# A hybrid DeltaNet, spatial-gating and Fourier step on one core: operations queued in written order, and the output's loads and end reordered

## The chip, the cores and the metric

The kernel runs on one core of one Trainium2 chip. The metric is the device time of one execution in microseconds (us). Its engines are TensorE (PE, its weight loads PEld), VectorE (DVE), ScalarE (ACT), GpSimd (POOL) and SyncE (SP), which only issues DMAs. Each engine works through a queue of its own in a fixed order, and waits on semaphores for the others.

## The reference

One layer of a backbone with three token mixers. It is run for 128 context tokens (the prompt) and 2048 latent tokens (the sample); `D_MODEL` is 1024, the branches are 512 wide, everything is float32.

```python
def mixer(xn, w_in, conv_w, ...):
    proj = jnp.einsum('btd,de->bte', xn, w_in)
    qkv, beta, dec, z_a, u_b, v_b, z_b, x_c, z_c, gates = jnp.split(proj, points, axis=-1)
    ...  # short conv and silu on qkv, l2norm of q and k, beta and decay
    o, s_f, s_b = delta_bidir(q, k, v, g, beta, s0_f, s0_b)   # chunks of 64, both directions
    o = rmsnorm(o, o_norm_g) * jax.nn.silu(z_a)
    o_b = chunk_sgu(u_b, v_b, sgu_norm_g, w_spatial, b_spatial) * jax.nn.silu(z_b)
    o_c = fourier_mix(x_c, grid) * jax.nn.silu(z_c)
    br = jnp.stack([o_a, o_b, o_c], axis=2)
    pb = jnp.einsum('btnw,nwd->btnd', br, w_branch)
    gt = jax.nn.sigmoid(gates.reshape(B, T, N_BRANCH, D_MODEL))
    merged = jnp.einsum('btnd,btnd->btd', gt, pb)
    return jnp.einsum('btd,de->bte', merged, w_out), s_f, s_b

def reference(...):
    # for each group: adaLN, xn = rmsnorm(h) * (1 + scale) + shift
    out, s_f, s_b = mixer(xn, ...)
    h = h + gate * out
    y = rmsnorm(h, final_g)
    # outputs: y_prompt, y_sample, the final states of the prompt's two scans
```

In `delta_bidir` each chunk needs the solution with a unit lower triangular matrix; the state is carried from chunk to chunk.

## The kernel before, in words

**Numbers.** Every large matrix product is three fp16 products: each operand is split into a high and a low part (`hi`, `lo`) after scaling by a power of two. A weight block is loaded as float32 (`wst`), then `converting` makes it: a square with a running sum on ScalarE (L309, whose elementwise result in `w.lo` is thrown away), a cast of the sum on VectorE (L258), a matmul with ones that spreads it over the partitions, the power of two from its exponent (L271 to L273, VectorE), the high part on ScalarE (L321) and the low part on VectorE (L322). The generator yields between these, so that other work is written in between. L309 occurs 81 times: 52 blocks of 1024 columns per partition, 24 branch blocks of 512, 4 blocks of the spatial branch and one small one.

**Stages.** In the trace: adaLN and the normalised input, up to 145 us; the qkv product with its convolution, to 410; the spatial branch's v, to 520; its u and z units, to 745; the Fourier branch, to 1045; then merges 1, 2 and 0 (a gate product, a branch product, a sigmoid and a sum each), to 1345, 1682 and 1986; the output product, final norm and stores, to the end. Beside these run, in pieces handed out by `pace` between the pieces of the large products, first the preparation of the delta branch (its decays, the chunk matrices, and `base_inverse`, called five times for up to four tiles of 128 tokens), from about 432 to 880 us, and then the scan of 33 steps, from about 880 to 1670.

**Order.** The framework plans the queue of each engine: it takes the program as written, simulates its time, and puts an instruction wherever its simulation finds the engine free and the operands ready. So an instruction can come to stand ahead of others that were written before it. `tc.issue_after(ins)` adds an edge: what is written inside comes after `ins` in that engine's queue. It is no wait, only an order. `_InTurn` wraps VectorE, ScalarE and TensorE; while its `kept` is set (some parts of the start and the end), every instruction gets an edge to the one written before it. `behind_gate` does the same for some ScalarE instructions of the merges, against a gate's activation.

**The inverse.** `base_inverse(g)` loads two halves of a matrix set (SP, L1097: `ndD`, written to DRAM by earlier steps), yields eight times, copies the second half to the other partitions with its axes exchanged (L1100, VectorE), and makes 31 pairs of VectorE operations (L1107, L1108). Its result goes to DRAM after a split (L1115, L1116). Steps of other tiles are written in between, among them VectorE's reads of PSUM banks (L1058, L1063, L1074, L1077) that TensorE's transposes (L1010) filled, and fill again when they are free.

**The scan.** A step takes the state `S`, splits it into fp16 parts (`split`, L1224 on ScalarE and L1225 on VectorE), multiplies, and hands the output to `attend`: four scaled copies out of PSUM on ScalarE (L1234), later four multiply-adds on VectorE (L1241). When a direction passes from the prompt to the sample, its state is replaced by the given one, which is scaled in place (L1342, VectorE, twice in all).

**The output.** Sixteen tiles of 128 rows are worked in eight pairs (`two_tiles`); a pair takes seven products of a quarter of the size instead of eight, with sums of operands and of weights (`tw[0]` to `tw[3]`, loaded by `sums_of`). Loads of this stage are issued by SP in an order fixed by `in_turn`. The last pair and the prompt's right half (`prompt_right`) are in strict written order: `squared` (ScalarE), `final` (times the final weights), `summed_up` (VectorE), `root` (GpSimd), then the scaling by the norm and the store.

Of the kernel before, what the change touches and what calls it, by code (L numbers as in the profile page):

```python
# [168 lines left out]
class _InTurn:  # L169


    def __init__(self, tc, engine):
        self.tc, self.engine, self.kept, self.last = tc, engine, False, None

    def __getattr__(self, name):
        f = getattr(self.engine, name)
        if not self.kept:
            return f

        def call(*args, **kw):  # L180
            with self.tc.issue_after(self.last.ins) if self.last is not None else ExitStack():
                self.last = f(*args, **kw)
            return self.last

        return call


@with_exitstack
def hybrid_flow_kernel(ctx: ExitStack, tc: tile.TileContext, x_prompt, x_sample, state_delta, c, c_ctx, w_ada,
# [3 lines left out]
    G, SY = nc.gpsimd, nc.sync  # L193
    V, A, PE = [_InTurn(tc, e_) for e_ in (nc.vector, nc.scalar, nc.tensor)]
# [102 lines left out]
    def converting(w, st, nkt, cols=P, hi=None, lo=None, tag="w", bufs=5, nth=0):  # L297
# [10 lines left out]
        with behind_gate():  # L308
            w.squared = A.activation(w.lo, st, AF.Square, accum_out=ss)  # L309
# [776 lines left out]
    def base_inverse(g):  # L1086
# [13 lines left out]
        V.tensor_copy(b3(X[64:P, :]), tmp[64:P, :].rearrange("p (i j) -> p j i", j=32))  # L1100
# [126 lines left out]
    def attend(d, t, S, u, qk_, qT_):  # L1227
        o = sb(dq, [P, WB], "o")
        if S is not None:
            ps = bank(ps_out, [P, WB])  # L1230
            for h in range(H):
                mm3(ps[:, hs(h)], pair(qT_, h), pair(S, h))
            for h in range(H):
                A.activation(o[:, hs(h)], ps[:, hs(h)], AF.Copy, scale=eg[:, d, t, h:h + 1])  # L1234
# [15 lines left out]
    def scan():  # L1250
# [31 lines left out]
        for i_, (d, s_, t) in enumerate(order):  # L1282
# [46 lines left out]
            if not last:  # L1329
# [7 lines left out]
                else:  # L1337
# [4 lines left out]
                    V.tensor_scalar(S2, S2, us, FS, ALU.mult, ALU.mult)  # L1342
# [651 lines left out]
    def two_tiles(t, pa, xr, hh, end):  # L1994
# [70 lines left out]

    parts = [sb(op, [P, 3], f"part{j}", bufs=1) for j in range(3)]
# [30 lines left out]
    def prompt_right():  # L2097
# [7 lines left out]
        final(gp_right, gp_right, cols[0], slice(512, 896), V)  # L2105
# [12 lines left out]
    ahead_rows = two_rows(firsts[0], in_turn)  # L2118
    sums_of(2)
    sums_of(0)  # L2120
    sums_of(3)
# [3 lines left out]
    for i, t in enumerate(firsts):  # L2125
        rows_ = ahead_rows
        if i < 7:
            ahead_rows = two_rows(firsts[i + 1], SY.dma_start if i else in_turn)
# [39 lines left out]
```

## Time and profile before

| | |
|---|---|
| three runs | 2155.57, 2153.13, 2153.15 us (median 2153.15) |
| the profiled execution | 2157.86 us, its span 2156.0 us |
| granted TensorE clock, mean over the span | 0.992 |
| TensorE busy | 2082.2 us (97%) |
| weight loads busy | 1195.7 us |
| VectorE busy | 1360.5 us (63%) |
| ScalarE busy | 1060.6 us (49%) |
| GpSimd busy | 758.3 us (35%) |

In the views, a row of the timeline is: start, duration, engine, line, operation, result <- operands, shapes, count, and in brackets the idle time of the engine before it with what ended that. "issue" means that the profile shows nothing that was waited for. A row of the waits is: engine and line, what it waited for, us in total, times, longest. A row of windows is: from:to, length, then busy time and count of PE, PEld, DVE, ACT and POOL, then the granted clock of TensorE (1.00 is full), the DMA engines' busy share, and GB/s.

### The profile page before, as it was taken

What the parts mean: (1) busy time and instruction counts of PE and PEld (TensorE: products, weight loads), DVE (VectorE), ACT (ScalarE), POOL (GpSimd) and SP (SyncE); (2) the same over time, 40 slices, a digit from 0 to 9 for tenths busy, and PEclk for the clock granted to TensorE, in tenths of its full rate; (3) what the DMA queues carried; (4) which work ended last, traced back from release to release, by engine and by line L of the source; (5) the groups of instructions that cost most, each with busy time, mean ns of one, the idle gap of its engine ahead of it and who ended that gap; (6) DMA issues with size and microseconds to landing.
All of it is one profiled execution on the core that took longest, in us unless ns stands there. A gap on an engine that the chain in (4) does not pass through costs nothing.

```text
span 2156.0 us, 42627 instructions
## 1 busy us (share of the span) xinstructions
PE 2082.2 (97%) x16133; PEld 1195.7 (55%) x16133; DVE 1360.5 (63%) x3100; ACT 1060.6 (49%) x2457; POOL 758.3 (35%) x934
## 2 busy tenths in 40 slices
PE   7999999999899999999899999999999999999997
PEld 4455444455455587778556556555655444444443
DVE  6656854389778698556755556766665554666245
ACT  5554744476565654445544445756554353443112
POOL 0321332233343322442421233355443234333464
PEclk9999999999999999999999999999999999999999
DMA  9625732277776744444755555866664645456852
GB/s 350 220 77 195 260 109 94 82 227 220 241 231 216 223 149 118 123 125 127 225 170 158 174 162 183 261 215 208 213 199 134 206 169 175 167 196 238 336 219 88
DMA packets 222910, 403.25 MB, mean 187 GB/s; under 512 B 39720, under 2 KB 109632, under 8 KB 219888
## 3 DMA queue, kind: packets, MB, share of 16 engines
q1 hardware_dynamic: 167664, 290.84, 42.3%
q0 software_dynamic: 15216, 65.89, 8.1%
q10 hardware_dynamic: 39824, 43.79, 6.1%
q8 instruction: 127, 2.08, 0.4%
q14 instruction: 79, 0.65, 0.1%
HBM read 258.19 MB, written 142.24 MB: 186 GB/s over the span
## 4 chain that ended last, share of the span: by engine, by line
PE 52%; DVE 9%; DMA 5%; ACT 3%; issue 2%; POOL 1%; SPq 0%; ACTq 0%; POOLq 0%; DVEq 0%
PE b L244 51%; DMA st<-br 2%; DVE XB L1107 1%; DVE E L1108 1%; DMA ei<-XB 1%; DMA tw<-tw 1%; DMA br<-o 0%; DMA XB<-nd 0%; DVE sg L1447 0%; DVE big L1684 0%; DMA N<-n 0%; ACT big L1683 0%; DVE XB L1116 0%; DVE n L1077 0%; DMA S<-in_state_delta_dram 0%
## 5 line engine op out<-in xcount | busy, mean ns | idle before, releaser
L244 PE MATMUL b<-xh,whi 128*128 128x512 f16 (+1 forms) x1920 | 649.8, 347 | 4.6 <-DVE sg L1447 2.8
L244 PE MATMUL b<-xl,whi 128*128 128x512 f16 (+1 forms) x1920 | 650.3, 347 | 0.0
L244 PE MATMUL b<-xh,wlo 128*128 128x512 f16 (+1 forms) x1920 | 649.3, 347 | 0.0
L244 PEld LDWEIGHTS <-whi 128*128 128x128 f16 x3856 | 351.1, 98 | 324.3 <-issue 10.4
L244 PEld LDWEIGHTS <-wlo 128*128 128x128 f16 x1928 | 188.4, 98 | 175.2 <-issue 1.3
L244 PE MATMUL b<-big,bhi 128*128 128x512 f16 (+1 forms) x960 | 251.8, 347 | 2.3 <-ACT big L1683 1.9
L244 PE MATMUL b<-big,blo 128*128 128x512 f16 (+1 forms) x480 | 163.1, 347 | 0.0
L1727 POOL TENSOR_TENSOR mrow<-mrow,sg 128x512 f32<-128x512 f32 (+1 forms) x80 | 92.5, 1157 | 147.2 <-DVE sg L1726 106.0
L244 PEld LDWEIGHTS <-xh 128*128 128x128 f16 x1496 | 118.8, 99 | 31.0 <-DVE yT L1633 2.7
L947 POOL TENSOR_TENSOR cy<-cy,raw 128x545 f32<-128x545 f32 (+1 forms) x48 | 65.8, 1398 | 181.2 <-ACT raw L946 181.2
L244 PEld LDWEIGHTS <-bhi 128*128 128x128 f16 x960 | 86.8, 98 | 75.0 <-issue 1.0
L244 PEld LDWEIGHTS <-xl 128*128 128x128 f16 x1068 | 98.9, 99 | 45.1 <-DMA tw<-tw 2.1
L1717 ACT ACTIVATE sg<-b,winv 128x512 f32<-128x512 f32 (+1 forms) x120 | 73.9, 616 | 92.8 <-PE b L244 92.2
L244 PE MATMUL b<-whi,xh 128*128 128x128 f16 x544 | 95.2, 222 | 3.3 <-DVE yT L1633 2.5
L244 PE MATMUL b<-wlo,xh 128*128 128x128 f16 x544 | 95.2, 222 | 0.0
L244 PE MATMUL b<-whi,xl 128*128 128x128 f16 x544 | 95.2, 222 | 0.0
L322 DVE SCALAR_TENSOR_TENSOR wlo<-wst,wsc,whi 128x1024 f16<-128x1024 f32 x52 | 68.1, 1310 | 33.5 <-ACT whi L321 32.5
L1181 POOL COPY T<-ES 32x256 f16<-32x256 f16 x68 | 30.8, 454 | 161.6 <-DMA ES<-ei 150.7
L1288 POOL TENSOR_TENSOR skn<-skn,ed 128x512 f32<-128x512 f32 x34 | 39.1, 1149 | 127.8 <-DMA skn<-kv 123.2
L321 ACT ACTIVATE whi<-wst,wsc 128x1024 f16<-128x1024 f32 x52 | 59.4, 1144 | 49.2 <-DVE wsc L272 47.4
L309 ACT ACTIVATE wlo<-wst 128x1024 f16<-128x1024 f32 x52 | 54.9, 1056 | 52.1 <-DMA wst<-in_w_blk_dram 47.2
L1726 DVE SCALAR_TENSOR_TENSOR sg<-b,binv,sg 128x512 f32<-128x512 f32 (+1 forms) x80 | 53.3, 667 | 39.9 <-PE b L244 35.9
(532 smaller groups left out, 4304.2 us busy)
## 6 DMA issues: line engine op xcount, KB each, us to landing
wst<-in_w_blk_dram SPq DMA_DIRECT2D x58, 512.0 KB, 3.8
pa<-pa POOLq DMA_DIRECT2D x16, 896.0 KB, 4.4
qkv<-cy POOLq DMA_DIRECT2D x12, 1089.0 KB, 5.3
st<-br SPq DMA_DIRECT2D x48, 256.0 KB, 3.2
mrow<-mrg SPq DMA_DIRECT2D x16, 576.0 KB, 3.9
pa<-pa SPq DMA_DIRECT2D x5, 1792.0 KB, 11.3
dc<-dec SPq DMA_DIRECT2D x17, 512.0 KB, 4.6
kq<-qkv SPq DMA_DIRECT2D x34, 256.0 KB, 4.5
```

Source lines behind the costliest of these rows:

```text
L244: newest[0] = PE.matmul(out, l, r, start=start, stop=stop, skip_group_check=reopened)
L309: w.squared = A.activation(w.lo, st, AF.Square, accum_out=ss)
L321: w.made = A.activation(w.hi, st, AF.Copy, scale=s)
L322: w.low = V.scalar_tensor_tensor(w.lo, st, s, w.hi, ALU.mult, ALU.subtract)
L947: G.tensor_tensor(y[:, c0:c1], y[:, c0:c1], raw[:, 1 + c0:1 + c1], ALU.mult)
L1107: V.tensor_tensor(t3, X3[:, 0:k, k:k + 1].to_broadcast([P, k, n_]), E3[:, k:k + 1, k:32].to_broadcast([P, k, n_]), ALU.mult)
L1108: V.tensor_tensor(E3[:, 0:k, k:32], E3[:, 0:k, k:32], t3, ALU.subtract)
L1181: G.tensor_copy(T16[rows(a0, b), :, :, b], ES[0:32, :, 2 * a0 + b, :, wT])
L1288: G.tensor_tensor(h3(kn_), h3(kn_), bc(ed[:, d, t, :], P), ALU.mult)
L1717: gated_[0] = A.activation(sg, ps, AF.Sigmoid, scale=gw.inv)
L1726: V.scalar_tensor_tensor(sg, ps, binv[:, 1:2], sg, ALU.mult, ALU.mult)
L1727: G.tensor_tensor(mr, mr, sg, ALU.add)
```

## The change

`_InTurn` now remembers the newest instruction written on its engine, always, and GpSimd is wrapped as well (nothing there is queued). `queued()` gives an edge to that newest instruction. Four places use it: the weights' squares (L309, ScalarE), the copy in `base_inverse` (L1100, VectorE), `attend`'s four scaled copies (L1234, ScalarE), and the scaling of the given state (L1342, VectorE). What is written after these instructions gets no edge to them.

In the output, SP's order of loads was sums 1, rows of the first pair, sums 2, sums 0, sums 3; it is now sums 1, 2, 0, the rows, sums 3. At the end, the last pair scales and stores only its row tile 1; tile 0 is scaled and stored in `prompt_right`, after the prompt's squares. `final` of the prompt's right half writes to a free buffer `f_` (another pair's) instead of in place, so it has no need to wait for ScalarE's squares of the same data, and both its parts come before the norm's root.

```diff
     def __getattr__(self, name):
         f = getattr(self.engine, name)
-        if not self.kept:
-            return f
 
         def call(*args, **kw):
-            with self.tc.issue_after(self.last.ins) if self.last is not None else ExitStack():
-                self.last = f(*args, **kw)
-            return self.last
+            with self.tc.issue_after(self.last.ins) if self.kept and self.last is not None else ExitStack():
+                self.newest = f(*args, **kw)
+            if self.kept:
+                self.last = self.newest
+            return self.newest
 
         return call
+
+    def queued(self):
+
+        return self.tc.issue_after(self.newest.ins) if self.newest is not None else ExitStack()
...
-        with behind_gate():
+        with behind_gate(), A.queued():
             w.squared = A.activation(w.lo, st, AF.Square, accum_out=ss)
...
-        V.tensor_copy(b3(X[64:P, :]), tmp[64:P, :].rearrange("p (i j) -> p j i", j=32))
+        with V.queued():
+            V.tensor_copy(b3(X[64:P, :]), tmp[64:P, :].rearrange("p (i j) -> p j i", j=32))
...
-            for h in range(H):
-                A.activation(o[:, hs(h)], ps[:, hs(h)], AF.Copy, scale=eg[:, d, t, h:h + 1])
+            with A.queued():
+                for h in range(H):
+                    A.activation(o[:, hs(h)], ps[:, hs(h)], AF.Copy, scale=eg[:, d, t, h:h + 1])
...
-                    V.tensor_scalar(S2, S2, us, FS, ALU.mult, ALU.mult)
+                    with V.queued():
+                        V.tensor_scalar(S2, S2, us, FS, ALU.mult, ALU.mult)
...
-        for j in (1, 0):
-            A.activation(hh[j], hh[j], AF.Copy, scale=norms[:, j:j + 1])
-            SY.dma_start(y_sample[0, (t + j) * P:(t + j + 1) * P], hh[j])
+        scaled(1, t)
+
+    def scaled(j, t):
+        h = last_rows[j]
+        A.activation(h, h, AF.Copy, scale=norms[:, j:j + 1])
+        SY.dma_start(y_sample[0, (t + j) * P:(t + j + 1) * P], h)
...
             squared(2, 1 + i, x_right, gp_right, cs)
-        final(gp_right, gp_right, cols[0], slice(512, 896), V)
+        scaled(0, firsts[-1])
+        f_ = room[:, (2 - 2 * nth[0]) * D:(2 - 2 * nth[0]) * D + 512]
+        for cs in cols:
+            final(f_, gp_right, cs, slice(512 + cs.start, 512 + cs.stop), V)
         summed_up(2, 1)
         summed_up(2, 2)
         root(2, 2)
-        final(gp_right, gp_right, cols[1], slice(896, D), V)
...
-        V.tensor_scalar(gp_right, gp_right, norms[:, 2:3], None, ALU.mult)
-        SY.dma_start(y_prompt[0, :, right], gp_right)
+        V.tensor_scalar(f_, f_, norms[:, 2:3], None, ALU.mult)
+        SY.dma_start(y_prompt[0, :, right], f_)
...
     sums_of(1)
-    ahead_rows = two_rows(firsts[0], in_turn)
     sums_of(2)
     sums_of(0)
+    ahead_rows = two_rows(firsts[0], in_turn)
     sums_of(3)
```

More of the change, by code (lines that the diff above doesn't have):

```diff
@@ L172, in __init__ @@
     def __init__(self, tc, engine):
[L173 removed]
+        self.tc, self.engine, self.kept, self.last, self.newest = tc, engine, False, None, None
     def __getattr__(self, name):
         f = getattr(self.engine, name)
[L177 to L178 removed]
         def call(*args, **kw):
[L181 to L185 removed]
+            with self.tc.issue_after(self.last.ins) if self.kept and self.last is not None else ExitStack():
[3 more added lines that the diff above has]
+            return self.newest
+        return call
+    def queued(self):
+        return self.tc.issue_after(self.newest.ins) if self.newest is not None else ExitStack()
 @with_exitstack
@@ L192, in hybrid_flow_kernel @@
     nc = tc.nc
-    G, SY = nc.gpsimd, nc.sync
-    V, A, PE = [_InTurn(tc, e_) for e_ in (nc.vector, nc.scalar, nc.tensor)]
+    SY = nc.sync
+    G, V, A, PE = [_InTurn(tc, e_) for e_ in (nc.gpsimd, nc.vector, nc.scalar, nc.tensor)]
     uid, rot = [0], [0]
@@ L2126, in hybrid_flow_kernel @@
         rows_ = ahead_rows
+        last_rows[:] = rows_[1]
         if i < 7:
```

1 line of the change is left out of this document (added).

## The prediction

> **What bounds the kernel now.** I read the page first, then the windows by stage, then the chain of waits grouped by engine, and last the timeline around each wait that the edited lines could be behind.
>
> ```profile
> span 2156.0 us, 42627 instructions
> PE 2082.2 (97%) x16133; PEld 1195.7 (55%) x16133; DVE 1360.5 (63%) x3100; ACT 1060.6 (49%) x2457; POOL 758.3 (35%) x934
> 162.00:540.00 378.00, 378.00 (x2270) 196.13 (x2269) 256.62 (x461) 208.07 (x411) 111.38 (x139) 1.00 0.51 170
> 540.00:1080.00 540.00, 504.31 (x5217) 351.89 (x5216) 396.61 (x1008) 290.98 (x796) 200.13 (x275) 0.98 0.58 178
> 1080.00:1998.00 918.00, 908.47 (x6949) 503.72 (x6947) 538.59 (x1324) 446.50 (x1050) 334.22 (x412) 1.00 0.59 191
> ```
>
> The columns of a window are its length, then busy time of PE, weight loads, VectorE, ScalarE, GpSimd, then the granted clock, the DMA share and GB/s. TensorE is the bound: 2156.0 - 2082.2 = 73.8 us of idle time is all that an edit of order can win, together with time at a reduced clock. Of it 35.7 us lie in 540 to 1080, 9.5 in 1080 to 1998, none in 162 to 540. The change touches no matmul, so every gain is a shorter TensorE wait or a shorter end, and anything it does before 540 can only cost.
>
> TensorE's waits, grouped by what ended them (us in total, times, longest):
>
> ```profile
> PE b L1010 <- issue: 6.3, 2, 4.8
> PE b L244 <- ACT S L1224: 4.7, 3, 2.3
> PE b L244 <- DVE yT L1633: 2.5, 1, 2.5
> PE b L244 <- ACT o L1234: 2.5, 2, 1.3
> PE b L244 <- DMA tw<-tw: 1.6, 1, 1.6
> ```
>
> Each of these five can be followed back to a line that the change edits. The rest of the table (other engines' results, a few tenths to 2.8 us each) has no edited line in front of it.
>
> **The inverse's copy (L1100, five times).** VectorE's timeline, with the TensorE rows that waited:
>
> ```profile
> 565.80 1.06 DVE L1100 COPY XB<-XB 64x1024 f32<-64x1024 f32 x1 [4.46 <-DMA XB<-nd]
> 568.99 0.63 PE L1010 MATMUL b<-cst,qr 128*128 128x128 f32 x4 [1.55 <-issue]
> 752.32 1.05 DVE L1100 COPY XB<-XB 64x1024 f32<-64x1024 f32 x1 [5.42 <-issue]
> 754.12 0.69 DVE L1074 TENSOR_TENSOR n<-b,dc 128x512 f32<-128x512 f32 x1
> 754.91 1.09 PE L1010 MATMUL b<-cst,qr 128*128 128x128 f32 x4 [4.77 <-issue]
> 833.28 1.06 DVE L1100 COPY XB<-XB 64x1024 f32<-64x1024 f32 x1 [3.69 <-DMA XB<-nd]
> 754.01:760.84 6.83, 5.92 (x52) 5.89 (x53) 6.46 (x23) 2.38 (x13) 3.27 (x6) 0.50 0.63 204
> ```
>
> The copy has been put ahead of work that was written before it, and its load has not landed. VectorE stands 4.46, 5.42 and 3.69 us in front of it in these three. Behind it in the queue is L1074, which reads a PSUM bank; TensorE's transposes (L1010) need that bank back. At 754.91 TensorE has stood for 4.77 us, at 568.99 for 1.55. With the edge, the copy can only be queued after the newest VectorE instruction that the program has written at that point. The operations written before it then run during those stands, and the two TensorE waits go: 4.77 + 1.55 = 6.3 us. The long wait has a second price: the window 754.01 to 760.84 is granted half the clock, with 5.92 us of busy TensorE in it, which is half of that, 3.0 us, at full clock. The other two of the five copies have no TensorE wait of this kind behind them. The sum is 9.3 us; its lower end is 0 (the place of the late bank is taken by something equally late, below). Its upper end is 11, with some tenths of waits by the inverse's own steps (L1043's transposes), which share VectorE with them. I take 9.3, since the waits are single and their cause is in the same queue.
>
> **The weights' squares (L309).** There are 81 of them, most ahead of their turn:
>
> ```profile
>   DMA wst<-in_w_blk_dram: 57.5, 27
> 1035.67 0.33 SPq L285 DMA_DIRECT2D wst<-in_w_brb_dram  x1
> 1039.39 0.63 ACT L309 ACTIVATE blo<-wst 128x512 f16<-128x512 f32 x1 [3.06 <-DMA wst<-in_w_brb_dram]
> 1040.02 0.61 ACT L1224 ACTIVATE S<-S 128x512 f16<-128x512 f32 x1
> 1040.68 0.24 PE L244 MATMUL b<-S,sk 128*128 128x128 f16 x1 [2.30 <-ACT S L1224]
> 1040.73:1044.15 3.42, 2.96 (x35) 2.88 (x35) 2.84 (x11) 3.37 (x9) 0.00 (x0) 0.50 0.46 153
> ```
>
> The first row is from what ended ScalarE's idle time in front of L309: 57.5 us, 27 times, for the weight's load. Nearly all of it is harmless, as TensorE shows no wait behind it. One is not: the square at 1039.39 waited for a load issued at 1035.67, the scan's state split (L1224) stood behind it, and TensorE 2.30 us behind that. Queued in its turn, the square comes after the split. That is 2.30 us, and half of the 2.96 us that TensorE was busy at half clock just after, 1.5: 3.8 us. The lower end is 0, the upper end 3.8 plus the rest of that wait's group, 4.7 - 2.3 = 2.4, so 6.2.
>
> [...]
>
> **S0's scaling (L1342).** It stands on VectorE for the state's load, ahead of the Fourier operations:
>
> ```profile
> 886.31 0.49 DVE L1342 TENSOR_SCALAR S<-S,usc 128x512 f32<-128x512 f32 x1 [3.15 <-DMA S<-in_state_delta_dram]
> 887.79 0.23 PE L244 MATMUL b<-whi,xh 128*128 128x128 f16 x1 [2.52 <-DVE yT L1633]
> 887.57 0.68 DVE L1225 SCALAR_TENSOR_TENSOR S<-S,S 128x512 f16<-128x512 f32 x1
> 929.44 0.74 DVE L1447 SCALAR_TENSOR_TENSOR sg<-b,zs,sg 128x512 f32<-128x512 f32 x1
> 929.92 0.83 PE L244 MATMUL b<-S,sk 128*128 128x128 f16 x12
> ```
>
> The 2.52 us wait goes. But the scaling is written only in the scan's first step, shortly before the matmul that reads its result at 929.92. In its turn it would start near 929.4, and scaling, ScalarE's half (0.61, as in the row at 1040.02) and VectorE's half take 0.49 + 0.61 + 0.68 = 1.8 us, so that matmul would be ready at 931.2, 1.3 us late. I count 2.5 - 1.3 = 1.2 us, with ends of 2.5 (TensorE has other work queued there) and 0. The second one, at the other direction's start, stands for nothing now and costs nothing.
>
> **Attention's copies (L1234).** TensorE's 2.5 us in two waits look like the aim, but in front of these two copies ScalarE waits for the store of the tile they overwrite, and the newest ScalarE instruction written is already ahead of them. The edge changes nothing there. I count 0; the lower end is a loss of 2.5 (the same group once more, where three other groups do move back), the upper end a gain of 2.5.
>
> **Output's loads.** The rows of the first pair go behind sums 2 and 0, so those sets come earlier on SP's one queue:
>
> ```profile
> 1986.41 0.85 SPq L1949 DMA_DIRECT2D tw<-tw  x2
> 2003.55 4.71 PE L244 MATMUL b<-tw,xl 128*128 128x512 f16 x21 [1.63 <-DMA tw<-tw]
> out_dram<-xh SPq DMA_DIRECT2D x16, 512.0 KB, 5.6
> ```
>
> The first row issues sums 0 and sums 3, and TensorE waits 1.63 us for sums 0. That wait goes, but sums 3, needed one product later (12 of those 21 matmuls, 2.7 us), still comes behind the same bytes as now and right after sums 0, so most of the 1.6 us reappears there. I count 0.2, with ends 0 and 1.6.
>
> **The end.** ScalarE scales both sample rows before it squares the prompt's last part:
>
> ```profile
> 2146.89 2.19 ACT L182 ACTIVATE xh<-xh,norms 128x1024 f32<-128x1024 f32 x2 [1.43 <-POOL norms L2083]
> 2148.99 0.51 ACT L182 ACTIVATE xl<-xl 128x384 f32<-128x384 f32 x1
> 2149.62 0.56 DVE L182 TENSOR_TENSOR xl<-xl,fg 128x384 f32<-128x384 f32 x1 [1.45 <-ACT xl L182]
> 2151.92 0.38 ACTq L182 DMA_DIRECT2D out_dram<-xh  x1
> ```
>
> One scaling, 2.19 / 2 = 1.1 us, moves behind the squares, and the multiplication by the final weights no longer waits 1.45 us for them. The prompt's last store is issued some 1.0 us earlier. The scaled sample row 0 is ready at 2146.89 + 2.19 = 2149.1 now; behind the two squares (0.51 us the first, the second no longer) it would be near 2150.1, and with the group's median of 5.6 us (last row of the fence before) its store could end at 2155.7, where the span ends now. So the ends are a gain of 1.0 and a loss of 1.0; I take a gain of 0.5, because little else is in flight by then.
>
> **The sum.** 9.3 + 3.8 + 1.2 + 0 + 0.2 + 0.5 = 15.0 us. Against it stands what becomes late next. The copy at 833.28 is in the last inverse; the newest VectorE work written then is a weight's low part:
>
> ```profile
> 842.07 1.28 DVE L322 SCALAR_TENSOR_TENSOR wlo<-wst,wsc,whi 128x1024 f16<-128x1024 f32 x1
> 864.00:918.00 54.00, 48.68 (x709) 41.94 (x708) 26.15 (x64) 24.26 (x55) 25.22 (x38) 0.97 0.46 124
> 1670.86 0.15 DVE L258 CAST bscb<-bss 128x1 bf16<-128x1 f32 x1
> 1682.81 0.17 PE L244 MATMUL b<-bscb,ones 128*128 128x1 bf16 x1
> ```
>
> In its turn the copy would start at 843.4, 10.1 us later, and with it the inverse's steps and the scan's first steps. In 864 to 918 TensorE already stands 5.3 us; the scan's matmuls are what fills the Fourier chain's waits there. Ten us less of them costs between 0 and another 5.3; I take 2.7. At its end the scan has 1682.81 - 1671.0 = 11.8 us in hand before merge 0 needs its scale, which holds the 10.1, but not much more. 15.0 - 2.7 = 12.3 us. The profiled execution took 2157.86 us (span 2156.0 and 1.9 around it), so it would take 2145.6. It lies 4.7 above the median of the three runs, 2153.15; the waits are waits of order and should be in every run, so I take the same 12.3 from the median: 2140.9, said as 2141.
>
> **Rivals.** *Half is given back.* Only the two largest waits (4.77 and 2.30) go without their clock terms, and 1 or 2 us reappear: a gain near 5, 2148. For it: the window from 754 is nearly full on VectorE (6.46 of 6.83 us), so freed work may collide there. Against it: the half clock follows both waits directly. *The stands only move*, or the edge does nothing because the newest written instruction had already been issued: a gain of 0 to 4, about 2151. For it: L1234, and the bulk of the 57.5 us that hides nothing. Against it: the 752 and 1040 rows have unfinished earlier work right behind the waiting instruction. *ScalarE's wait becomes VectorE's.* The cast behind each square is not queued:
>
> ```profile
> DVE wscb L258 <- ACT wlo L309: 82.0, 32, 7.4
> ```
>
> VectorE already stands 82.0 us there. A later square with an unmoved cast adds up to 57.5 / 27 = 2.1 us to each stand, and the scan's and Fourier's splits are behind it. If one in three of the 81 squares reached TensorE at 0.85 us, that is 23 us against the 15: 2161. It decides from about 19 us of new TensorE waits on (15 eaten, 4 more to be seen). Against it: the casts follow the squares by their data, and the order is planned with that in view; TensorE has almost none of its idle time behind L258 now, in spite of the 82.0. *More than the sum*: the waits' groups go whole, 18 to 20 us, 2134.
>
> **Numbers.** Forecast (gain 8 to 16) 0.52; half given back 0.20; stands only move 0.13; VectorE's wait, slower, 0.12; more than the sum 0.03. About 0.2%, 4.3 us, is what a measurement of this kernel can tell from no change. Faster by more: 0.52 + 0.03 + 0.16 of the half case = 0.71. Same: 0.13 + 0.04 = 0.17. Slower 0.12. The range reaches from the largest sum, 2134, to 2154, where the stands merely move; it leaves out the slow case and little else.
>
> **What would show it.** Right: no VectorE idle time of 3 to 5 us in front of L1100; no L1010 wait ended by "issue" near 755 and full clock from 754 to 761; no wait of the 887 transform for L1633; the scan's split ahead of the square near 1040; the row-0 scaling after the prompt's squares at the end. Wrong: TensorE's idle time in 540 to 1080 still near 35 us, new waits for L322, L258 or L1225, a wait for sums 3 near 2005, or idle time at the end of merge 2 near 1683.

## The result and the profile after

The changed kernel took 2173.6 us (median of 4 runs, 2169.3 to 2178.0), the kernel before 2154.4 in the same session: a ratio of 1.0079 with a 95% interval of 1.0062 to 1.0096, 17 us slower. The forecast was 12 us faster. The profiled execution took 2172.59 us.

In the changed kernel, and in every kernel below, the operations of four engines go through the helper that knows `newest`, so they all show its line, L180. They are read by tile and time from here on. First the page and the windows of the profile after (window, length, busy time of PE, weight loads, VectorE, ScalarE, GpSimd, granted clock, DMA share, GB/s):

```profile
span 2170.8 us, 42614 instructions
PE 2090.4 (96%) x16133; PEld 1197.5 (55%) x16133; DVE 1372.7 (63%) x3100; ACT 1061.5 (49%) x2457; POOL 752.0 (35%) x934
162.00:275.00 113.00, 106.68 (x583) 52.42 (x582) 87.07 (x84) 69.80 (x92) 33.22 (x34) 0.98 0.68 236
702.00:810.00 108.00, 105.63 (x1057) 74.07 (x1055) 92.68 (x241) 70.22 (x213) 37.97 (x50) 1.00 0.60 188
1940.00:1998.00 58.00, 55.52 (x305) 26.99 (x304) 37.24 (x70) 24.66 (x42) 22.73 (x24) 0.97 0.50 177
```

The same three windows of the kernel before:

```profile
162.00:275.00 113.00, 113.00 (x622) 55.48 (x621) 82.57 (x81) 68.71 (x90) 31.86 (x34) 1.00 0.66 228
702.00:810.00 108.00, 102.75 (x1027) 74.15 (x1025) 87.67 (x229) 67.45 (x204) 36.08 (x48) 0.97 0.60 184
1940.00:1998.00 58.00, 58.00 (x297) 27.37 (x296) 34.84 (x60) 22.51 (x38) 21.95 (x23) 1.00 0.68 249
```

TensorE's instructions are the same 16133. Its idle time rose from 73.8 to 2170.8 - 2090.4 = 80.4 us, and its busy time by 8.2 us, part of it at a lower clock (mean granted clock 0.990, before 0.992). In 702 to 810 the gain that was forecast is there: 5.3 us idle became 2.4, and the clock is full. The loss begins where the prediction had said that nothing could be won: 162 to 275 had no idle time, and now has 6.3 us of it and 39 matmuls fewer. Later windows of merges add to it: 1940 to 1998 was full and has 2.5 us of idle time and a clock of 0.97. In 540 to 1100, where the gains were sought, the idle time fell only from 36.8 to 33.3 us.

Where the time goes can be read from single matmuls that have the same number of matmuls ahead of them in both traces. The one with 1633 ahead of it starts at 282.18 us, 7.8 us later than before; with 10862 ahead, at 1345.23, 5.8 us later; with 14528 ahead, at 1842.07, 11.4 later; the last one 15.4 later. So 7.8 us are lost by 282 us, some 2 are won back by 1345, 5.6 are lost up to 1842 and 4.1 behind that.

TensorE's and VectorE's waits after, grouped by what ended them (us in total, times, longest):

```profile
PE b L180 <- DVE wscb L180: 7.2, 3, 3.3
PE b L180 <- issue: 1.6, 2, 1.3
DVE wscb L180 <- ACT wlo L180: 44.7, 23, 8.4
```

The first row is new: the matmul of a weight's scale waits for the cast of the weight's sum of squares. The waits by "issue" fell from 7.6 us (6.3 and 1.3 on two lines of the kernel before) to 1.6, and the one near 755 is gone. VectorE stands less in front of these casts than before, 44.7 us and not 82.0.

### The profile page after: what moved, and what is told of

It is laid out like the page before. It is cut to its first block, busy times and chain, and to the rows that moved or that the text cites. A ratio compares the mean times of both kernels' runs of the same rounds, so it can differ in the third digit from the quotient of the medians.

```text
span 2170.8 us, 42614 instructions
## 1 busy us (share of the span) xinstructions
PE 2090.4 (96%) x16133; PEld 1197.5 (55%) x16133; DVE 1372.7 (63%) x3100; ACT 1061.5 (49%) x2457; POOL 752.0 (35%) x934
## 4 chain that ended last, share of the span: by engine, by line
PE 47%; DVE 6%; DMA 5%; ACT 2%; issue 2%; POOL 1%; SPq 0%; ACTq 0%; DVEq 0%; POOLq 0%
PE b L180 47%; DMA st<-br 2%; DVE sg L180 1%; DMA tw<-tw 1%; DVE XB L180 1%; DMA wst<-in_w_ada_dram 1%; DVE big L180 0%; DVE X L180 0%; DVE yT L180 0%; DVE S L180 0%; DVE xh L180 0%; ACT big L180 0%; DVE n L180 0%; DMA wst<-gate 0%; DVE sv L180 0%
## 5 line engine op out<-in xcount | busy, mean ns | idle before, releaser
L180 PE MATMUL b<-xh,whi 128*128 128x512 f16 (+1 forms) x1920 | 653.2, 349 | 6.1 <-DVE sg L180 5.8
L180 PE MATMUL b<-xl,whi 128*128 128x512 f16 (+1 forms) x1920 | 653.3, 349 | 0.0
L180 PE MATMUL b<-xh,wlo 128*128 128x512 f16 (+1 forms) x1920 | 651.9, 348 | 0.0
L180 PEld LDWEIGHTS <-whi 128*128 128x128 f16 x3888 | 357.9, 98 | 340.5 <-issue 22.5
L180 PEld LDWEIGHTS <-wlo 128*128 128x128 f16 x1944 | 191.0, 98 | 173.5 <-issue 3.8
L180 PE MATMUL b<-big,bhi 128*128 128x512 f16 (+1 forms) x960 | 251.1, 348 | 3.8 <-ACT sg L180 2.4
L180 ACT ACTIVATE sg<-b,winv 128x512 f32<-128x512 f32 (+1 forms) x180 | 110.6, 617 | 146.6 <-PE b L180 137.0
L180 PE MATMUL b<-big,blo 128*128 128x512 f16 (+1 forms) x480 | 163.7, 348 | 0.0
L180 POOL TENSOR_TENSOR mrow<-mrow,sg 128x512 f32<-128x512 f32 (+1 forms) x80 | 96.5, 1208 | 136.0 <-DVE sg L180 103.8
L180 PEld LDWEIGHTS <-xh 128*128 128x128 f16 x1496 | 118.2, 99 | 30.5 <-DVE yT L180 3.2
L180 POOL TENSOR_TENSOR cy<-cy,raw 128x545 f32<-128x545 f32 (+1 forms) x48 | 66.4, 1410 | 188.7 <-ACT raw L180 188.7
L180 PEld LDWEIGHTS <-bhi 128*128 128x128 f16 x960 | 87.2, 98 | 78.9 <-issue 3.3
L180 PEld LDWEIGHTS <-xl 128*128 128x128 f16 x1068 | 98.7, 98 | 45.9 <-DMA tw<-tw 1.7
L180 POOL COPY T<-ES 32x256 f16<-32x256 f16 x68 | 28.1, 414 | 211.5 <-DMA ES<-ei 183.5
L180 PE MATMUL b<-whi,xh 128*128 128x128 f16 x544 | 94.4, 221 | 2.9 <-DVE yT L180 2.9
L180 PE MATMUL b<-whi,xl 128*128 128x128 f16 x544 | 94.4, 221 | 0.0
L180 PE MATMUL b<-wlo,xh 128*128 128x128 f16 x544 | 94.4, 221 | 0.0
L180 DVE SCALAR_TENSOR_TENSOR wlo<-wst,wsc,whi 128x1024 f16<-128x1024 f32 x52 | 70.9, 1363 | 34.8 <-ACT whi L180 34.7
L180 DVE SCALAR_TENSOR_TENSOR sg<-b,binv,sg 128x512 f32<-128x512 f32 (+1 forms) x80 | 53.2, 667 | 48.4 <-PE b L180 45.8
L180 ACT ACTIVATE whi<-wst,wsc 128x1024 f16<-128x1024 f32 x52 | 59.5, 1144 | 48.5 <-DVE wsc L180 46.5
L180 ACT ACTIVATE raw<-b,winv 128x512 f32<-128x512 f32 (+1 forms) x60 | 36.7, 619 | 88.1 <-PE b L180 86.8
L180 POOL TENSOR_TENSOR skn<-skn,ed 128x512 f32<-128x512 f32 x34 | 37.0, 1089 | 107.7 <-DMA skn<-kv 102.6
```

The costliest lines, as they stand in the source:

```text
L180: self.newest = f(*args, **kw)
```

## The experiments

Each kernel below is the kernel before with the named edges only. `queued()` is the method of the diff. The helper alone moves none of TensorE's work: in output_only, which has none of the four edges, the 16133 matmuls stand in the order of the kernel before. Times are medians against the kernel before in the same session, with the 95% interval of the ratio. A trace is of one execution, and where its time is far from the median the text says so. The theory that the profile after suggested: the squares' edge takes away a lead that their results had before TensorE needs them, and the matmul of the weight's scale waits. The rivals: another edge costs, the copy's by giving back, the scan's, or the output's loads; or the cast behind the square on VectorE is what is late, and not the square.

**The parts.** Four kernels split the change.

```diff
# all_but_squares: the whole change, but
-        with behind_gate(), A.queued():
+        with behind_gate():
# squares_only: this edge and nothing else
+        with behind_gate(), A.queued():
# copy_only
+        with V.queued():
             V.tensor_copy(b3(X[64:P, :]), ...)
# output_only: the order of the two rows' loads, and the new end
```

> The change without the edge on the weights' squares (L309); the other five parts stay. Theory A (the squares' edge costs what was lost: in its turn a square comes late, VectorE's cast and TensorE's ones-matmul behind it come later still, and TensorE's queue stands for them): no waits of TensorE for wscb at 216 and 260, the wait near 755 still gone, 2145 to 2151 us, faster than before. Rival B (the copy's edge costs, by starting inverses and scan later): 2163 to 2175, as the whole change. Rival C (each edge makes the order of everything else anew, by a few us either way): 2150 to 2163, with new waits in 540 to 1430 that belong to no edited line.

> The kernel before with the edge on the weights' squares alone. Theory A: 2166 to 2178 us, with TensorE's waits for wscb (3.3 and 3.0 us at 216 and 260, with half the clock behind them) as in the changed kernel, and the 4.8 us wait near 755 back. Rival B: within 4 us of 2154. Rival C: slower, but by waits elsewhere than at wscb.

> The kernel before with the edge on the inverse's copy (L1100) alone. Theory A and the prediction's step: the waits at 569 and 755 with their half clock go, 9 us, less up to 3 given back: 2145 to 2149 us. Rival B: 2160 or more, with the scan's first steps some 10 us later and waits in 864 to 1080. Rival C: 2149 to 2158, the 9 us eaten by waits that the new order makes elsewhere.

> The kernel before with the output's part alone: loads reordered, end reordered. All theories: nothing before 1980 us moves; a gain of 0 to 2 us (predicted 0.7), 2152 to 2155, too little for the times to show; the profile decides by the wait for the sums near 2003 and by the time from TensorE's last matmul to the end (12.4 us before, in the changed kernel to be compared).

| kernel | median us | ratio |
|---|---|---|
| all_but_squares | 2162.5 | 1.0017 (1.0005 to 1.0028) |
| squares_only | 2173.8 | 1.0086 (1.0067 to 1.0105) |
| copy_only | 2153.1 | 0.9975 (0.9963 to 0.9986) |
| output_only | 2159.7 | 1.0010 (0.9999 to 1.0020) |

The squares alone cost what the whole change costs. The copy is a gain of 0.0025 x 2157 = 5.4 us. What is left of the change beside the squares is slower too, in spite of the copy, so another edge costs as well.

The copy's windows and rows in copy_only:

```profile
702.00:810.00 108.00, 106.26 (x1091) 75.82 (x1090) 91.30 (x243) 71.06 (x217) 39.03 (x54) 1.00 0.62 196
755.64 1.05 DVE L180 COPY XB<-XB 64x1024 f32<-64x1024 f32 x1
836.05 1.04 DVE L180 COPY XB<-XB 64x1024 f32<-64x1024 f32 x1 [3.66 <-DMA XB<-nd]
```

The copy that stood 5.42 us at 752.32 now starts at 755.64 with no wait; the window has 1.7 us of idle time instead of 5.3, 64 matmuls more, and the full clock. The one at 833.28 moved only 2.8 us, to 836.05, and still stands 3.66 us for its load. Not all is gain: a wait of 2.56 us by "issue" stands at 586.76 in front of the same transposes, where the kernel before had none of this kind.

**The first stage.** The squares of the weights that are used before 540 (the first 21 of 81), those of the merges (from the 38th on), and those between them, apart; `nsq` counts the calls.

```diff
+        nsq[0] += 1
-        with behind_gate():
+        with behind_gate(), A.queued() if nsq[0] <= 21 else ExitStack():   # squares_early
+        with behind_gate(), A.queued() if nsq[0] >= 38 else ExitStack():   # squares_merges
+        with behind_gate(), A.queued() if 22 <= nsq[0] <= 37 else ExitStack():   # squares_middle
```

> The kernel before with the edge on the squares of the first weights only: those used before 540 us (the qkv product's twelve and the spatial branch's four). It changes the order of almost nothing after 540. Theory A (a square in its turn on ScalarE makes the cast on VectorE late, and TensorE stands for the ones-matmul behind it): +5 to +8 us, waits for wscb at about 217 and 260 and half the clock behind them, nothing else. Rival C (the loss is the new plan's, spread over the whole kernel): within 2 us of the kernel before.

> The kernel before with the edge on the merges' 48 squares only (used from 1049 us on). Theory A in its strict form (waits at wscb): 1 to 3 us slower, as only one such wait (0.85 us near 1050) was seen there. Rival C (the new plan's waits, not at wscb, 4 us each in 1350 to 1404 and in 1944 to 1998): 6 to 12 us slower. If both hold, this and the early ones add up to the 18 us of squares_only.

> The edge on the 16 squares between the early ones and the merges' (u, z and Fourier weights, used from 525 to 1045 us). If the parts of squares_only add up (0.86 = 0.38 + 0.24 + this): 1.002 to 1.003. If they do not (the early delay is partly what costs later): 0.999 to 1.001.

squares_early took 2167.8 us (1.0038, 1.0025 to 1.0051), squares_merges 2163.3 (1.0024, 1.0008 to 1.0040), squares_middle 2156.8 (1.0000, 0.9988 to 1.0013). The parts make 0.38 + 0.24 + 0.00 = 0.62%; the 0.86% of all squares is not clear of that sum within the intervals.

What the early part does is read at the tenth weight. The kernel before, square, cast, matmul of its scale (start, length, engine):

```profile
176.10 1.05 ACT L309 ACTIVATE wlo<-wst 128x1024 f16<-128x1024 f32 x1
184.50 0.15 DVE L258 CAST wscb<-wss 128x1 bf16<-128x1 f32 x1
208.08 0.17 PE L244 MATMUL b<-wscb,ones 128*128 128x1 bf16 x1
```

The kernel after, the same three, with VectorE's queue between them:

```profile
209.26 0.69 ACT L180 ACTIVATE raw<-b,winv 128x512 f32<-128x512 f32 x1
209.84 1.05 ACT L180 ACTIVATE wlo<-wst 128x1024 f16<-128x1024 f32 x1
212.62 1.21 DVE L180 TENSOR_TENSOR E<-E,cst 128x1024 f32<-128x1024 f32 x1
213.75 2.47 DVE L180 SCALAR_TENSOR_TENSOR cy<-raw,pc,cy 128x2178 f32<-128x2178 f32 x1
216.15 0.14 DVE L180 CAST wscb<-wss 128x1 bf16<-128x1 f32 x1
216.34 0.16 PE L180 MATMUL b<-wscb,ones 128*128 128x1 bf16 x1 [3.34 <-DVE wscb L180]
```

Before, the square ran 34 us earlier and the matmul found its operand 208.08 - 184.65 = 23.4 us old. (The eleventh and twelfth weights had less, 6.6 and 1.8 us.) With the edge the square stands behind an eviction of the current block and starts at 209.84. Behind it the cast takes its place in VectorE's queue after operations of 1.21 and 2.47 us, and the matmul, written for this place among TensorE's own, waits 3.34 us with every later matmul behind it: none starts between 212.79 and 216.34. Squares_early shows the same: its group "wscb" is 6.8 us in three waits, at 217.52, 235.53 and 260.21. The matmul of the thirteenth weight's scale, with 1633 matmuls ahead of it in both kernels, before and in squares_early:

```profile
274.34 0.17 PE L244 MATMUL b<-wscb,ones 128*128 128x1 bf16 x1
283.98 0.17 PE L180 MATMUL b<-wscb,ones 128*128 128x1 bf16 x1
```

It is 9.6 us later, and the whole span is 10.0 us longer. So what this execution lost was lost by 284 us: 6.8 us in the three waits, 1.7 by one stretch of half clock (260.39 to 263.80; the mean granted clock over 210 to 275 is 0.97), and some 1 us that is not traced.

**Is it the cast or the square?** In early_squares_scalar_cast the cast goes to ScalarE, right behind its square, so VectorE's queue is out of the way.

```diff
+        if 6 <= nsq[0] <= 21:
+            sb16 = sb(wp, [P, 1], "wscb", BF16)
+            A.copy(sb16, ss)
+        else: ...   # widened(...) as before, on VectorE
```

> As squares_early (edge on the squares used before 540 us), but the cast behind each of the qkv product's and the spatial branch's squares is made on ScalarE right behind the square instead of on VectorE (the same numbers, 16 short operations more on ScalarE). Theory A (VectorE's queue between square and ones-matmul makes it late): the waits for wscb near 217, 235 and 260 (3.4, 1.0, 2.4 us) and the half clock go, most of the 8 us come back: 0.999 to 1.001 of the kernel before. Rival A2 (the square itself is too late in ScalarE's queue): the waits stay, 1.002 to 1.004.

It took 2168.3 us (1.0066, 1.0050 to 1.0081), slower than squares_early (1.0038). ScalarE's timeline around the twelfth weight:

```profile
260.45 1.06 ACT L180 ACTIVATE E<-tok 128x1024 f32<-128x1024 f32 x1 [1.79 <-DMA tok<-in_state_delta_dram]
261.51 0.67 ACT L180 ACTIVATE raw<-b,winv 128x512 f32<-128x512 f32 x1
262.08 1.04 ACT L180 ACTIVATE wlo<-wst 128x1024 f16<-128x1024 f32 x1
263.25 0.19 ACT L180 CAST wscb<-wss 128x1 bf16<-128x1 f32 x1
263.49 0.16 PE L180 MATMUL b<-wscb,ones 128*128 128x1 bf16 x1 [4.98 <-ACT wscb L180]
```

The cast is right behind its square now, and the wait is longer, 4.98 us, with 1512 matmuls ahead as before. Here it is the square that is late: it stands behind an operation that waits for the state's load, and behind the eviction in front of it. So VectorE's cast alone is not the cost. That it adds nothing is not shown: in the kernel after, 5.2 us of VectorE's queue lie between the tenth square's end and its cast, and this variant has costs of its own (VectorE stands 8.7 us once for a cast on ScalarE).

**Take the cause away at three weights, or give the chain more time.** In early_without_three, weights 10, 11 and 12 have no edge. In early_one_step_later they have it, and their scale's matmul is written one piece of work later.

```diff
+        with behind_gate(), A.queued() if nsq[0] <= 21 and not 10 <= nsq[0] <= 12 else ExitStack():   # without_three
+        if 10 <= n_ <= 12:
+            yield          # one_step_later, ahead of scales(...)
```

> squares_early (1.0038) with the edge taken off three of its squares, those at 211, 233 and 257 us, behind which TensorE stood for the ones-matmul (3.4, 1.0, 2.4 us). Theory A: the loss is theirs alone: 0.9995 to 1.0010, no waits for wscb. If the loss is spread, or the next squares become late instead: 1.002 to 1.004.

> squares_early with all its edges, but for those three weights the ones-matmul and all behind it are written one piece of the large product later (about 11 us of TensorE's queue); in the queue only the first of the three moves. If what is missing is time between the square and the ones-matmul: the 3.4 us wait at 217 and its half clock go, the other two stay, 1.001 to 1.0025. If the waits are set by something else that TensorE needs: 1.003 to 1.005.

early_without_three took 2161.0 us (1.0019, 1.0006 to 1.0032): by the ratios half the loss of squares_early is gone with three edges of 21, though the two intervals overlap from 1.0025 to 1.0032. The waits at 217 to 260 are gone with it, but the next weight with the edge takes their place:

```profile
273.36 1.06 ACT L180 ACTIVATE wlo<-wst 128x1024 f16<-128x1024 f32 x1
274.38 5.08 DVE L180 SCALAR_TENSOR_TENSOR cy<-raw,pc,cy 128x2178 f32<-128x2178 f32 x2
279.37 0.15 DVE L180 CAST wscb<-wss 128x1 bf16<-128x1 f32 x1
279.58 0.16 PE L180 MATMUL b<-wscb,ones 128*128 128x1 bf16 x1 [4.05 <-DVE wscb L180]
```

early_one_step_later took 2162.3 us (1.0020, 1.0006 to 1.0034); its profiled execution is one of the faster ones, 2157.9. It came out the other way round than expected: the wait at 217 stayed, with 3.84 us, and those at 235 and 260 went. The matmuls ahead of each scale's matmul tell why. For the tenth weight they are 1295 in squares_early and here too, so this one was not moved. For the eleventh and twelfth they are 1415 and 1536 here, and were 1391 and 1512: these two stand 24 places later and wait no more. The thirteenth, again with 1633 ahead, now waits 1.09 us. So this is shown for this stage: the edge takes away the lead that the chain square, cast, matmul needs, and the waits come and go with that lead, weight by weight. That the lost time goes with them fits both ratios, within their intervals.

**The merges' squares.** They don't wait at the scale's matmul. The window and one of TensorE's waits in squares_merges, and a second wait (last row) from merge 2:

```profile
1940.00:1998.00 58.00, 55.66 (x277) 25.97 (x276) 32.76 (x56) 20.55 (x36) 21.06 (x22) 0.97 0.68 249
1965.47 1.33 ACT L180 ACTIVATE pa<-sums,msc 128x512 f16<-128x512 f32 x2 [0.85 <-DVE sums L180]
1966.71 0.92 ACT L180 ACTIVATE sg<-b,winv 128x512 f32<-128x512 f32 x2
1967.43 0.27 PE L180 MATMUL b<-big,bhi 128*128 128x128 f16 x2 [2.25 <-ACT sg L180]
1371.84 0.27 PE L180 MATMUL b<-u,kn 128*128 128x128 f16 x1 [3.15 <-ACT u L180]
```

Here no square is in sight. The activation that TensorE waits for is behind two splits that wait for sums; edges elsewhere have changed the order that the planner writes for ScalarE. The window had no idle time before. Both waits stand in the kernel after too (2.39 us at 1983.92, 2.58 us at 1386.20).

The profiled execution took only 2156.8 us, as it reached merge 2 early: the matmul with 10862 ahead of it starts at 1331.05, before at 1339.48. From there to the last matmul it lost 7.4 us against the kernel before, 3.4 of them ahead of 1725.80 and 4.0 behind 1825.71. The second part is what the wait at 1967.43 and the half clock behind it make (2.25 us, and half of the 3.42 us from 1969.02). In the first part stands the wait at 1371.84, with half clock from 1371.69 to 1378.52 (the mean over 1344 to 1440 is 0.96). By the medians the edges cost 0.24%, 5.2 us.

**The scan's two edges.** S0's scaling and attention's copies together, then apart; then attention's groups apart, to find the place (`nat` counts the groups).

```diff
+            with A.queued():                        # attend_only
                 for h in range(H): A.activation(o[...], ps[...], AF.Copy, ...)
+            with A.queued() if nat[0] <= 1 else ExitStack():   # attend_first_group
+            with A.queued() if nat[0] > 3 else ExitStack():    # attend_other_groups
+            with A.queued() if nat[0] == 6 else ExitStack():   # attend_sixth_group
+                    with V.queued():                # state_scaling_only
                         V.tensor_scalar(S2, S2, us, FS, ALU.mult, ALU.mult)
```

> The kernel before with the edges on S0's scaling (L1342) and attend's copies (L1234) only. By subtraction (all_but_squares 1.0017 less copy_only 0.9975) they cost 0.4%, 9 us: 1.003 to 1.005, with the wait for the scaled state's split near 930 that the prediction put at 1.3 us, more waits in 864 to 1100, and the transform's 2.5 us near 887 gone. By the prediction's steps they gain 1.2 us: 0.999 to 1.000. Rival C: anything within 0.3% either way, with waits that belong to neither line.

> The kernel before with the edge on S0's scaling (L1342) alone. If this is what made scan_edges_only slow (1.0037): 1.002 to 1.004, the transform's wait near 887 gone (2.5 us) but a wait for the split of S near 930 (1.1 us) and the scan's steps bunched, with waits for Q at 950 (1.5 and 1.7 us). By the prediction's step: 0.999 to 1.000.

> The kernel before with the edge on attend's scaled copies (L1234) alone. By the prediction's step (nothing moves but three groups): 0.999 to 1.001. If it is what made scan_edges_only slow: 1.002 to 1.004, with the wait of 3.7 us near 1050 (split of S behind the copies and the weight's square) and 1.9 us for o near 1094.

> The edge on attend's copies for the first of the 32 groups only. In attend_only its copies ran at 963.5 us instead of 943.0, and the products that need the same bank (u times sqk) at 965.9 instead of 944.8. If that is the cost: 1.001 to 1.002, TensorE's extra loss in 918 to 1026 (some 4 us) without that in 1080. Otherwise within 0.05% of before.

> The edge for the groups from the fourth on only; in attend_only the sixth group's copies ran at 1086.9 us, in the kernel before at 1050.2, with TensorE waiting 2.1 us for them at 1088. If that group is the cost: 1.001 to 1.002, the extra loss in 1026 to 1134 (some 4 us) without that in 918 to 1026. Both this and the first group should add up to attend_only's 1.0032.

> The edge on attend's copies for the sixth of the 32 groups only. If its place behind the conversions of merge 1's operand is the cost: 1.002 to 1.003, copies near 1085, TensorE waiting about 2 us for them; if the cost comes from the new plan around 1018 to 1040 (other groups): 1.000 to 1.001.

| kernel | median us | ratio |
|---|---|---|
| scan_edges_only | 2168.0 | 1.0037 (1.0025 to 1.0049) |
| state_scaling_only | 2157.6 | 1.0005 (0.9993 to 1.0017) |
| attend_only | 2163.3 | 1.0032 (1.0017 to 1.0047) |
| attend_first_group | 2158.1 | 1.0002 (0.9989 to 1.0015) |
| attend_other_groups | 2163.3 | 1.0029 (1.0011 to 1.0048) |
| attend_sixth_group | 2157.6 | 1.0002 (0.9990 to 1.0015) |

S0's scaling costs and gains nothing that can be measured: the 2.52 us wait at 887 is gone, and the split is late at the scan's first matmul, as these rows of state_scaling_only show:

```profile
925.51 0.62 DVE L180 TENSOR_SCALAR S<-S,usc 128x512 f32<-128x512 f32 x1
927.85 0.22 PE L180 MATMUL b<-S,sk 128*128 128x128 f16 x1 [1.12 <-ACT S L180]
```

Attention's edge is the second cost of the change, 0.32%. Between the matmuls with 6671 and 8807 ahead of them (919.68 and 1115.97 us before) attend_only's execution lost 9.1 us against the kernel before, and behind them nothing; output_only, with TensorE's order of before, lost 2.3 there. In attend_only the scan's split near 1040 shows how the place moves:

```profile
1040.01 0.63 ACT L180 ACTIVATE blo<-wst 128x512 f16<-128x512 f32 x1 [4.20 <-DMA wst<-in_w_brb_dram]
1040.63 0.61 ACT L180 ACTIVATE sg<-st 128x512 f32<-128x512 f32 x1
1041.25 0.61 ACT L180 ACTIVATE S<-S 128x512 f16<-128x512 f32 x1
1041.91 0.22 PE L180 MATMUL b<-S,sk 128*128 128x128 f16 x1 [3.82 <-ACT S L180]
```

Between the square that waits for its load and the split stands a square (of another tile, `st`) that was not there before, and ScalarE stands longer for the load (4.20 us, before 3.06); TensorE's wait of 2.30 us became 3.82. The cost is in the groups from the fourth on (1.0029); the first group's copies alone, 24.7 us later than before, cost nothing that can be measured. In attend_other_groups the sixth group's copies, at 1050.23 before, stand behind conversions that wait for loads, and TensorE waits for them in the execution that was profiled:

```profile
1080.89 0.40 ACT L180 ACTIVATE big<-st,bsc 128x128 f16<-128x128 f32 x1 [1.61 <-DMA st<-br]
1082.27 0.81 ACT L180 ACTIVATE big<-st,bsc 128x128 f16<-128x128 f32 x2 [0.40 <-DMA st<-br]
1082.99 1.12 ACT L180 ACTIVATE o<-b,eg 128x128 f32<-128x128 f32 x4
1084.16 0.83 PE L180 MATMUL b<-u,sqk 128*128 128x128 f16 x12 [2.17 <-ACT o L180]
```

That place had been my theory for the loss. In attend_sixth_group, which has the edge there alone, the same wait stands:

```profile
1092.01 0.83 PE L180 MATMUL b<-u,sqk 128*128 128x128 f16 x12 [2.12 <-ACT o L180]
```

Its time is that of the kernel before, 1.0002, so the theory fell: this group's edge alone costs nothing that can be measured. Which of the order's other changes between 919 and 1116 us costs the 0.3% is open. These two traces can't tell: the one of attend_other_groups is of an execution of 2156.6 us, as fast as the kernel before (six of its twelve took 2154.0 to 2160.5, the other six 2166.1 to 2168.6), and the one of attend_sixth_group is of the longest of twelve, 2167.4.

**The best of it.** The copy's edge and the output's order, and the same with the edge on one square, the one that stood at 1039.39 in the kernel before:

```diff
+        with V.queued():                            # both: copy, and output's order and end
             V.tensor_copy(b3(X[64:P, :]), ...)
+        with behind_gate(), A.queued() if nsq[0] == 41 else ExitStack():   # copy_output_one_square
```

> The kernel before with the inverse's copy queued and the output's two edits, nothing else. If parts add up: copy_only's 0.9975 and output_only's 1.001 make 0.997 to 0.999, 2151 to 2155 us on this scale. If S0's scaling and attend's copies are harmless, and what made all_but_squares slow (1.0017) is an interplay of copy and output, this is 1.001 or more.

> A version that may beat both: copy_and_output (0.9968), and the edge on a single square, the one that stood for its load at 1039 in the kernel before (the second branch block of merge 1). If the prediction's reading of that place is right (2.3 us of wait and 1.5 us of half clock): 0.9950 to 0.9960, with no wait for the split of S there. If the wait is only passed on to the ones-matmul or the branch product behind it: 0.9965 to 0.9980.

They took 2152.5 us (0.9968, 0.9957 to 0.9978) and 2149.8 us (0.9970, 0.9959 to 0.9981). Both beat the kernel before by 0.3% and the kernel after by 1%, and can't be told apart. In the second the split stands ahead of the square, as the prediction had it, and TensorE waits for the next thing:

```profile
1030.43 0.63 ACT L180 ACTIVATE S<-S 128x512 f16<-128x512 f32 x1 [0.54 <-DVE S L180]
1034.70 0.61 ACT L180 ACTIVATE blo<-wst 128x512 f16<-128x512 f32 x1
1036.26 0.84 PE L180 MATMUL b<-S,sq__1574_13738 128*128 128x128 f16 x12 [1.85 <-DMA sq__1574_13738<-qT]
```

## Why the prediction was wrong, by its steps

One reading on the way was off, and nothing hung on it: the rest of the table of waits, "a few tenths to 2.8 us each", has rows of 3.6, 3.5 and 3.0 us.

- **The inverse's copy (+9.3, less 2.7): right in kind, near in size.** Alone it is worth 5.4 us (3.0 to 8.0 by the interval) against 6.6. The 755 wait and the half clock behind it went (the mean clock over 702 to 810 is 1.00 in copy_only, before 0.97). The give-back was mis-sized in its parts: the last inverse's copy moved 2.8 us and not 10.1, and the cost showed instead as a 3.2 us wait for the scan's N near 896 and the 2.56 us at 586.76. The 4.77 us that carried the term came from one execution. In kernels that leave this copy as it was, that wait was 1.3 us (squares_merges), 2.0 (attend_only), 3.8 (squares_only) and 5.1 (output_only), so it was no sure 4.77 either. In all of these but squares_only, TensorE's order up to there is that of the kernel before.
- **The squares (+3.8): this is the step that failed.** They cost 0.0086 x 2157 = 18.6 us. The prediction took the 57.5 us of ScalarE's waits for loads as "nearly all harmless", since TensorE showed no wait behind them, and looked for gain at one place; the other 80 squares stood at nothing. It did not ask what those early squares were buying. In the first stage it was the lead between the cast and the matmul that needs it, 23.4 us at the tenth weight. The edge spent it, and squares_early lost 9.6 us there. In the merges the waits are of another kind: the edges changed the order around them. The text itself said that anything before 540 can only cost, and then priced that at nothing. The one place it did price was right as far as it went: with that square alone queued the 2.30 us wait is gone, and 1.85 us of another stands in its stead; the time is the same within the noise (0.9970 against 0.9968).
- **The rival that came true, and its mechanism.** The prediction's signs of being wrong included new waits for L258; that one came. The slower rival, at 2161, named the unmoved cast behind each square, but its price was VectorE's stand of 82.0 us growing. That stand shrank to 44.7. The time was lost on TensorE, where every later matmul stands behind the scale's matmul (3.34 us at 216.34 after), and moving the cast to ScalarE did not help.
- **S0's scaling (+1.2): right in kind.** The 2.52 us wait went and a wait of 1.12 us came where it was forecast (1.3); net, 0.0005 (-0.0007 to 0.0017) shows no gain, but holds the forecast one (1.2 us is 0.0006) as well.
- **Attention's copies (0): wrong.** They cost 0.32%, 6.9 us, beyond the 2.5 that stood as the lower end. The text held that the edge "changes nothing there", from the two groups whose wait it had seen. The groups from the fourth on do move, and with them other instructions' places in the plan, and the time goes between 919 and 1116 us; which of these moves costs it stays open.
- **Loads and end (+0.7): right in size where it can be seen,** from the start of the last matmul to the end 12.60 us became 11.64 in output_only and 11.96 after, and the wait for sums 0 fell from 1.63 to 1.19. The whole kernel's 1.0010 (0.9999 to 1.0020) doesn't show it. The end after:

```profile
2163.39 0.51 ACT L180 ACTIVATE xl<-xl 128x384 f32<-128x384 f32 x1
2164.18 1.81 ACT L180 ACTIVATE xh<-xh,norms 128x1024 f32<-128x1024 f32 x2
2166.03 0.38 ACTq L180 DMA_DIRECT2D out_dram<-xh  x1
```

The parts measured alone, 0.86 for the squares, 0.32 for attention, 0.05 for S0 and -0.32 for the copy and the output together, add up to 0.91%, against 0.79 for the whole, which the intervals allow. Each kind of edge moves more than its own line. Compared place by place, with matmuls of the same tiles and shapes taken as equal, TensorE's order differs from that of the kernel before in 789 of 16133 places in copy_only, in 871 in attend_only and in 4903 in squares_only.

## What to carry to other kernels

Work that runs far ahead of its turn, and stalls its own engine on the way, may be paying for a lead elsewhere (23.4 us at the tenth weight; without it TensorE waited 3.34 us): before putting it "in its turn", follow its result to the last in-order queue that holds a consumer, and compare the lead there with the new delay. That TensorE shows no wait behind an idle engine's waits does not make them harmless to move: ScalarE's 57.5 us had almost none behind them, and the edge on the first 21 squares cost 0.38%. And where a planner writes the order, one new edge can move much that it does not name: measure each kind of edge alone. Even on the one instance that shows a wait it may only pass the wait on, as the single square here did (2.30 us went, 1.85 us came).

## What the runs showed of the hardware

In squares_merges the wait of 2.25 us at 1967.43 is the only one of over 1 us in 1940 to 1998. The clock ahead of its end and behind it:

```profile
1960.00:1967.00 7.00, 5.18 (x42) 3.05 (x41) 4.15 (x9) 2.86 (x6) 2.67 (x3) 1.00 0.62 239
1967.00:1971.00 4.00, 3.48 (x20) 1.72 (x20) 1.98 (x4) 0.96 (x3) 3.04 (x5) 0.75 0.94 284
1969.02:1972.44 3.42, 3.42 (x10) 1.22 (x9) 1.74 (x3) 1.41 (x3) 3.21 (x4) 0.50 0.85 336
```

The clock was full until 1969.02, half for 3.42 us and full again (0.82 in the mean over 1971 to 1975); the 0.75 is a mean over both. The prediction's row for 1040.73 shows the same 0.50 for 3.42 us behind a wait of 2.30 us. In the kernel after, TensorE waits 2.98 us ahead of 260.09, and the clock stays at 1.00 from there to 271.00. What sets the clock here is not shown.

A visible wait is no fixed size either: the one near 755 took 4.77 us in the kernel before, 5.11 in output_only and 1.29 in squares_merges, with TensorE's order up to there the same in all three.
